# Moving low parts of weights and pooling operands from GpSimd to VectorE in a hybrid decoder layer

## The chip, the cores and the metric

The kernel runs on one core of one Trainium2 chip. The metric is the device time of one execution in microseconds. A core has five engines with instruction queues of their own, each worked off strictly in order: TensorE (PE, matrix products; PEld is its loading of weights), VectorE (DVE), ScalarE (ACT), GpSimd (POOL), and SyncE (SP), which here issues most transfers. An engine whose next instruction waits for another engine holds up everything behind that instruction.

## The reference

One decoder layer over 1024 tokens of width 1024, all in float32:

```python
z = h @ w_in                                   # split into pool group | q | k | v
y_pool = pool_mixer(u_pool, w_pool, pool_scale)
y_attn = sliding_window_attention(q, k, v, sinks)   # window 128, 8 query heads, 2 kv heads
mix = concat([y_pool, y_attn]) @ w_out
h = layer_norm(ALPHA * h + mix, ln1_g, ln1_b)
ff = square(relu(h @ w_ff1)) @ w_ff2
h = layer_norm(ALPHA * h + ff, ln2_g, ln2_b)
h = h + sigmoid(h @ w_ple_gate + b) * (p @ w_ple)

def pool_mixer(u, w_pool, pool_scale):         # four groups of 128 channels, windows 2, 4, 8, 16
    d = mean of the last `window` tokens - u   # fewer tokens at the sequence's start
    return (d @ w_pool[group]) * pool_scale
```

## The kernel before

Every float32 product is made of three fast ones. An operand is split into a high part, its value rounded to the matrix engine's own format, and a low part, the rest; `mm3` adds high x high, high x low and low x high. The high part is made by ScalarE (`high`, line 98, a copy with rounding) and the low part by `low` (line 103), a subtraction `source - high`, on an engine that the caller names. So a low part comes always after a cast by ScalarE.

Tokens lie in two halves of 512 (t = 0, 1). The first 300 us of the program hold these stages, interleaved:

- The input projection (`z_tile`): each block of 128 columns of `w_in` is loaded into a staging tile `st` (two buffers), split into `w` (two buffers), and multiplied with eight blocks of x.
- `attention(n)` for eight blocks of 128 queries, in two groups of heads each: scores (lines 289, 290, tile s), bias and row minimum on VectorE (line 293, tile e), exponential on ScalarE (line 300), reciprocal (304) and scaling (306) on VectorE, transposes (313, tile pt), split into pp, product with the values (318, 319, tile av), sum of its halves (321, 322, tile y), split into the `mixA` tiles (c). The low part of `mixA` is GpSimd's.
- `pooling`: for four groups in each half, the window sums (line 357, up to four additions of 512 to 527 columns) on GpSimd, the difference to the token (line 360, tile h) on VectorE, in the first half the correction of the first tokens (lines 365, 366) on GpSimd, then the split of the operand `dT` (tile `tmp`, one buffer) and its product with the group's matrix `wp`. The result is scaled into `mixP` (lines 100, 376).
- The output projection's left half of columns for the first four token blocks (`out_left(0, ...)`): its weights come in four pieces of 128x1024, staged in st and split into w (w_1757, w_1786, w_1815, w_1844 in the rows below); four accumulators (mm_1753 to mm_1755 and s_1756) take all eight k blocks, and `residual` (line 437) adds them to the residual rows n. Then the right half's weights `wo` (c_1984 and c_1993, two pieces each) for `out_right`, and `out_left(1, ...)`, whose weights (w_2118, w_2147 and two more) are split by VectorE already.

Then come the first layer norm (lines 399 to 415), the feed-forward layer as fewer block products (from about 300 us on), and the gate.

The order of the instructions on each engine is made by a scheduler that plays the program with its own estimates of durations when it is built; code order only breaks ties. A change of engine therefore moves other instructions too. Buffers are few: of the accumulators `mm` there are three, and a new one waits until an old one's reader is through.

Of the kernel before, what the change touches and what calls it, by code (L numbers as in the profile page):

```python
# [12 lines left out]
P = 128  # L13
D = 1024
S = 1024
HALF = 512
# [51 lines left out]
def layer(ctx, tc, xT, x, pT, w_in, w_pool, pscale, sinks, w_out, ln1, w1, w2, ln2, w_ple, w_gate, bgate, bias, rcount, out):  # L68
    nc = tc.nc
# [6 lines left out]
    def nm(s):  # L76
        uid[0] += 1
        return f"{s}_{uid[0]}"

    def big(shape, dt=F32R):  # L80
        return sb.tile(shape, dt, tag="c", bufs=6, name=nm("c"))

    def wt(shape, dt=F32R):
        return sb.tile(shape, dt, tag="w", bufs=2, name=nm("w"))
# [4 lines left out]
    def stage(shape):  # L89
        return sb.tile(shape, F32, tag="st", bufs=2, name=nm("st"))  # L90
# [5 lines left out]
    def high(dst, src, scale=None):  # L96
        if scale is None:
            nc.scalar.copy(out=dst, in_=src)  # L98
        else:
            nc.scalar.mul(out=dst, in_=src, mul=scale)  # L100

    def low(eng, dst, src, hi):
        return eng.tensor_tensor(out=dst, in0=src, in1=hi.bitcast(F32), op=ALU.subtract)  # L103

    def load_split(dst_h, dst_l, src, shape, eng, st=None):
        st = stage(shape) if st is None else st
        nc.sync.dma_start(out=st, in_=src)
        high(dst_h, st)
        low(eng, dst_l, st, dst_h)

    def mm3(o, ah, al, bh, bl, first, last, more=False):
        nc.tensor.matmul(o, ah, bh, start=first, stop=False, skip_group_check=more)  # L112
        nc.tensor.matmul(o, ah, bl, start=False, stop=False, skip_group_check=more)  # L113
        nc.tensor.matmul(o, al, bh, start=False, stop=last, skip_group_check=more)  # L114
# [30 lines left out]
    def tmp(shape, dt=F32):  # L145
        return pa.tile(shape, dt, tag="tmp", bufs=1, name=nm("tmp"))

    def row(shape, dt=F32):
        return pa.tile(shape, dt, tag="h", bufs=6, name=nm("h"))
# [14 lines left out]
    def acc_ps():  # L164
        return ps.tile([P, HALF], F32, tag="mm", bufs=3, name=nm("mm"))
# [172 lines left out]
    def pooling(n):  # L338
        for _ in range(n):
            while steps and len(ahead) < 2:  # L340
                gi, t = steps.pop(0)
                ahead.append((gi, t, z_tile(6 + gi, t)))
            pool_group(*ahead.pop(0))

    def pool_group(gi, t, o):
        win = WINDOWS[gi]
        u = row([P, PAD + HALF])
        nc.gpsimd.tensor_copy(out=u[:, 0:PAD], in_=halo[:, gi, :])
        nc.scalar.copy(out=u[:, PAD:], in_=o)
        if t == 0:  # L350
            nc.gpsimd.tensor_copy(out=halo[:, gi, :], in_=u[:, HALF : HALF + PAD])
        sums = [row([P, PAD + HALF]) for _ in range(2)]
        cur, a, side = 1, u, 0
        while cur < win:
            d0 = 2 * cur - 1
            b = sums[side]
            nc.gpsimd.tensor_tensor(out=b[:, d0:], in0=a[:, d0:], in1=a[:, d0 - cur : PAD + HALF - cur], op=ALU.add)  # L357
            a, side, cur = b, 1 - side, 2 * cur
        dd = sums[side][:, PAD:]
        nc.vector.scalar_tensor_tensor(  # L360
            out=dd, in0=a[:, PAD:], scalar=1.0 / win, in1=u[:, PAD:], op0=ALU.mult, op1=ALU.subtract
        )
        if t == 0:
            f = win - 1
            nc.gpsimd.tensor_tensor(out=dd[:, 0:f], in0=a[:, PAD : PAD + f], in1=rc[:, 0:f], op=ALU.mult)
            nc.gpsimd.tensor_tensor(out=dd[:, 0:f], in0=dd[:, 0:f], in1=u[:, PAD : PAD + f], op=ALU.subtract)
        dT = tmp([P, 2, HALF], F32R)
        high(dT[:, 0], dd)
        low(nc.gpsimd, dT[:, 1], dd, dT[:, 0])
        y = acc_ps()  # L370
        mm3(y, wp[:, 0, gi, :], wp[:, 1, gi, :], dT[:, 0], dT[:, 1], True, True)
        if mixP[t] is None:
            mixP[t] = big([P, 2, 4, HALF])
        m = mixP[t]
        high(m[:, 0, gi, :], y, psc[:, gi : gi + 1])
        nc.vector.scalar_tensor_tensor(
            out=m[:, 1, gi, :], in0=y, scalar=psc[:, gi : gi + 1], in1=m[:, 0, gi, :].bitcast(F32),
            op0=ALU.mult, op1=ALU.subtract,
        )
# [47 lines left out]
    def out_load(dst, dh, kk, st, eng):  # L427
        load_split(dst[:, 0], dst[:, 1], w_out[dh, kk], None, eng, st)

    def out_mm(o, n, k, w):  # L430
        m = (mixP if k < 4 else mixA)[n // 4]
        c = (n % 4) * P
        mm3(o, m[:, 0, k % 4, c : c + P], m[:, 1, k % 4, c : c + P], w[:, 0, k % 2, :], w[:, 1, k % 2, :], k == 0, k == NK - 1)
# [6 lines left out]
    def out_left(t, staging, eng, room=None):  # L440
        blocks = range(4 * t, 4 * t + 4)
        os = [acc_ps() for _ in range(3)]
        os.append(ps.tile([P, HALF], F32, tag="s", bufs=2, name=nm("s")))
        for k in range(NK):
            if k % 2 == 0:
                w = room[:, k // 2 - 2] if room is not None and k > 3 else wt([P, 2, 2, HALF])
                out_load(w, 0, k // 2, staging(), eng)
            for n in blocks:
                out_mm(os[n % 4], n, k, w)
        return os  # L450

    def residual_load(t):
        for n in range(4 * t, 4 * t + 4):
            hn[n] = nat([P, D])
            nc.sync.dma_start(out=hn[n], in_=x[n * P : (n + 1) * P, :])
# [35 lines left out]
    attention(6)  # L491
    pooling(2)
    residual_load(0)
    left = out_left(0, lambda: stage([P, 2, HALF]), nc.gpsimd)
    attention(7)
    residual_left(0, left)
    pa_ctx.close()
# [95 lines left out]
    for j in range(2):  # L593
        w = big([P, 2, 2, 2, HALF])
        for i in range(2):
            out_load(w[:, i], 1, 2 * j + i, stage([P, 2, HALF]), nc.gpsimd)
        wo.append(w)
    gb1 = [stage([P, D]) for _ in range(2)]
    for j in range(2):
# [368 lines left out]
```

## Time and profile before

| what | value |
|---|---|
| median of 3 runs | 1004.0 us (1003.68 to 1005.26) |
| profiled execution | 1003.74 us, span 1001.9 us, mean granted TensorE clock 0.996 |
| TensorE busy | 989.8 us (99%) |
| VectorE busy | 709.4 us (71%) |
| ScalarE busy | 459.0 us (46%) |
| GpSimd busy | 129.2 us (13%), 158 instructions |

In the profile, a line such as `L103 POOL TENSOR_TENSOR tmp<-h,tmp 128x512` is one group or one instruction: the source line (that of the helper `low`, so the tile's name tells which split it is), the engine, the operation, output and inputs, and partitions by elements. What stands in square brackets in a timeline is the idle time of that engine before the instruction and what ended it. In a row of waits, "PE av L319 <- DVE pp L103: 2.8, 2, 2.5" says that TensorE waited for VectorE 2.8 us in all, twice, 2.5 at the longest.

### The profile page before, as it was taken

How to read it: one execution, taken by the hardware profiler on the slowest of the kernel's cores; microseconds unless marked ns; L12 is line 12 of the kernel's file. 1: busy time of each engine (PE TensorE's matmuls, PEld its weight loads, DVE VectorE, ACT ScalarE, POOL GpSimd, SP SyncE). 2: the span in 40 equal slices, each digit the busy share in tenths (PEclk: the TensorE clock that was granted, in tenths of full speed). 3: DMA queues.
4: the chain of work that ended last, by engine and by line, in shares of the span. 5: the costliest groups of instructions: out<-in, count | busy, mean ns of one | idle time of the engine just before them, and what ended most of it. 6: DMA issues, size and time to landing. Idle time of an engine off the chain costs nothing.

```text
span 1001.9 us, 12220 instructions
## 1 busy us (share of the span) xinstructions
PE 989.8 (99%) x4562; PEld 822.2 (82%) x4562; DVE 709.4 (71%) x1121; ACT 459.0 (46%) x737; POOL 129.2 (13%) x158
## 2 busy tenths in 40 slices
PE   9999998999999999999999999999999999999998
PEld 7888886788888888888888888888888888888887
DVE  5889897666878876666446756887657699897333
ACT  5667766542576444344454433433433354651111
POOL 0031655430000000100000000100021110000000
PEclk9999998999999999999999999999999999999999
DMA  6524111452152433663264793775798773621011
GB/s 216 179 75 156 44 64 63 148 167 85 74 198 107 165 150 123 199 173 135 87 235 162 299 335 114 176 231 190 204 225 187 201 168 126 200 85 43 32 43 43
DMA packets 39004, 148.01 MB, mean 148 GB/s; under 512 B 4768, under 2 KB 5920, under 8 KB 36128
## 3 DMA queue, kind: packets, MB, share of 16 engines
q1 hardware_dynamic: 29952, 116.29, 33.6%
q0 software_dynamic: 7840, 26.74, 11.5%
q10 hardware_dynamic: 1152, 4.19, 1.0%
q8 instruction: 36, 0.59, 0.2%
q14 instruction: 24, 0.20, 0.1%
HBM read 124.66 MB, written 22.54 MB: 147 GB/s over the span
## 4 chain that ended last, share of the span: by engine, by line
PE 91%; DVE 5%; ACT 2%; POOL 1%; issue 1%; DMA 1%; SPq 0%; ACTq 0%; DVEq 0%; POOLq 0%
PE f L112 22%; PE f L114 22%; PE f L113 22%; PE mm L113 6%; PE mm L114 6%; PE mm L112 6%; DVE e L306 1%; PE pt L313 1%; PE f L424 1%; DVE e L293 1%; DVE pp L103 1%; POOL h L357 1%; PE av L319 1%; DMA n<-in_xT 1%; DVE h L360 1%
## 5 line engine op out<-in xcount | busy, mean ns | idle before, releaser
L112 PE MATMUL f<-c,ws 128*128 128x512 f32 (+1 forms) x456 | 175.8, 385 | 0.0
L113 PE MATMUL f<-c,ws 128*128 128x512 f32 (+1 forms) x456 | 175.7, 385 | 0.0
L114 PE MATMUL f<-c,ws 128*128 128x512 f32 (+1 forms) x456 | 175.2, 385 | 0.0
L113 PE MATMUL f<-x,w 128*128 128x512 f32 x448 | 174.3, 389 | 0.0
L114 PE MATMUL f<-x,w 128*128 128x512 f32 x448 | 174.3, 389 | 0.0
L112 PE MATMUL f<-x,w 128*128 128x512 f32 x448 | 147.1, 389 | 0.0
L98 ACT CAST w<-st 128x1024 fp32r<-128x1024 f32 (+2 forms) x66 | 65.7, 998 | 105.9 <-issue 69.8
L103 DVE TENSOR_TENSOR w<-st,w 128x1024 fp32r<-128x1024 f32 (+2 forms) x62 | 72.9, 1178 | 46.1 <-ACT w L98 46.0
L114 PEld LDWEIGHTS f<-c,ws 128*128 128x128 f32 x456 | 85.7, 188 | 17.2
L112 PEld LDWEIGHTS f<-c,ws 128*128 128x128 f32 x456 | 85.7, 188 | 17.1
L113 PEld LDWEIGHTS f<-c,ws 128*128 128x128 f32 x456 | 85.7, 188 | 17.0
L113 PEld LDWEIGHTS f<-x,w 128*128 128x128 f32 x448 | 84.1, 188 | 17.6
L114 PEld LDWEIGHTS f<-x,w 128*128 128x128 f32 x448 | 84.1, 188 | 17.4
L112 PEld LDWEIGHTS f<-x,w 128*128 128x128 f32 x448 | 84.1, 188 | 17.3
L98 ACT CAST ws<-w 128x512 fp32r<-128x512 f32 x60 | 37.1, 622 | 58.0 <-PE f L114 42.4
L103 DVE TENSOR_TENSOR x<-ws,x 128x1024 fp32r<-128x1024 f32 x52 | 63.4, 1219 | 0.0
L103 DVE TENSOR_TENSOR ws<-w,ws 128x512 fp32r<-128x512 f32 x60 | 41.2, 689 | 28.6 <-ACT ws L98 28.2
L117 DVE TENSOR_TENSOR n<-t,f 128x512 f32<-128x512 f32 x48 | 31.9, 685 | 39.3 <-PE f L114 39.2
L113 PE MATMUL mm<-c,w 128*128 128x512 f32 x144 | 56.9, 396 | 0.3 <-DVE c L103 0.3
L112 PE MATMUL mm<-c,w 128*128 128x512 f32 x144 | 56.7, 400 | 0.0
L114 PE MATMUL mm<-c,w 128*128 128x512 f32 x144 | 56.5, 395 | 0.0
L98 ACT CAST ws<-st 128x512 fp32r<-128x512 f32 x48 | 29.8, 621 | 58.1 <-PE f L114 35.2
(214 smaller groups left out, 1850.9 us busy)
## 6 DMA issues: line engine op xcount, KB each, us to landing
ws<-in_w SPq DMA_DIRECT2D x70, 512.0 KB, 3.6
w<-in_w SPq DMA_DIRECT2D x16, 1024.0 KB, 5.0
c<-fd SPq DMA_DIRECT2D x6, 2048.0 KB, 8.6
fd<-n POOLq DMA_DIRECT2D x20, 512.0 KB, 4.2
ws<-in_w POOLq DMA_DIRECT2D x20, 512.0 KB, 7.5
st<-in_w_in SPq DMA_DIRECT2D x17, 512.0 KB, 3.3
w<-in_w SPq DMA_DIRECT2D x10, 512.0 KB, 3.8
n<-in_x SPq DMA_DIRECT2D x8, 512.0 KB, 4.3
```

The lines of the kernel that those rows point to most:

```text
L98: nc.scalar.copy(out=dst, in_=src)
L103: return eng.tensor_tensor(out=dst, in0=src, in1=hi.bitcast(F32), op=ALU.subtract)
L112: nc.tensor.matmul(o, ah, bh, start=first, stop=False, skip_group_check=more)
L113: nc.tensor.matmul(o, ah, bl, start=False, stop=False, skip_group_check=more)
L114: nc.tensor.matmul(o, al, bh, start=False, stop=last, skip_group_check=more)
L117: nc.vector.tensor_tensor(out=o, in0=a, in1=b, op=op)
L293: nc.vector.tensor_tensor_reduce(out=e[:, 2 * j + i, k0 : 2 * P], in0=s[:, i, k0 : 2 * P], in1=nd[:, k0 : 2 * P], scale=-SLOPES[h], scalar ...
L306: nc.vector.tensor_scalar(out=e[:, i, k0 : 2 * P], in0=e[:, i, k0 : 2 * P], scalar1=st[:, 12 + i : 13 + i], scalar2=None, op0=ALU.mult)
L313: nc.tensor.transpose(pt[:, i, :], e[:, i, kb * P : (kb + 1) * P], ident)
L319: nc.tensor.matmul(av, VV[0][:, blk, g], pp[:, 1], start=False, stop=(kb == 1))
L357: nc.gpsimd.tensor_tensor(out=b[:, d0:], in0=a[:, d0:], in1=a[:, d0 - cur : PAD + HALF - cur], op=ALU.add)
L360: nc.vector.scalar_tensor_tensor(out=dd, in0=a[:, PAD:], scalar=1.0 / win, in1=u[:, PAD:], op0=ALU.mult, op1=ALU.subtract)
```

## The change

The engine of three groups of low parts is another: those of the pooling operands (eight of 128x512), of the weights of `out_left(0, ...)` (four of 128x1024) and of the right half's weights `wo` (four of 128x1024). GpSimd keeps the low parts of `wp` and of `mixA`, the window sums and the small copies.

```diff
@@ pool_group
         high(dT[:, 0], dd)
-        low(nc.gpsimd, dT[:, 1], dd, dT[:, 0])
+        low(nc.vector, dT[:, 1], dd, dT[:, 0])
@@ 
-    left = out_left(0, lambda: stage([P, 2, HALF]), nc.gpsimd)
+    left = out_left(0, lambda: stage([P, 2, HALF]), nc.vector)
@@ 
-            out_load(w[:, i], 1, 2 * j + i, stage([P, 2, HALF]), nc.gpsimd)
+            out_load(w[:, i], 1, 2 * j + i, stage([P, 2, HALF]), nc.vector)
```

The scheduler makes another order of it. Three places on VectorE show it. The first is a pooling group of the first half (h_1138 is the token tile, h_1142 its window sum, h_1143 the difference, tmp_1150 its split; e_1160 is an attention tile; w_1329 an input weight). Before:

```order
L322 TENSOR_TENSOR y_791<-av_868,yl_889 64x512
L103 TENSOR_TENSOR pp_997<-pt_992,pp_997 128x512
L360 SCALAR_TENSOR_TENSOR h_1143<-h_1142,h_1138 128x512
L103 TENSOR_TENSOR pp_1007<-pt_1002,pp_1007 128x512
L293 ISA e_1160,sm_1161<-s_1162,nd,sink_sb 128x256
```

and now:

```order
L322 TENSOR_TENSOR y_791<-av_868,yl_889 64x512
L103 TENSOR_TENSOR pp_1007<-pt_1002,pp_1007 128x512
L360 SCALAR_TENSOR_TENSOR h_1143<-h_1142,h_1138 128x512
L103 TENSOR_TENSOR tmp_1150<-h_1143,tmp_1150 128x512
L103 TENSOR_TENSOR w_1329<-st_1330,w_1329 128x1024
L293 ISA e_1160,sm_1161<-s_1173,nd,sink_sb 128x256
```

The low part of tmp_1150 stands directly behind the difference from which ScalarE must first make the high part; two groups of the second half (tmp_1521, tmp_1570) stand so too, and the other five have other work in between.

The second place is the end of the pooling, where the output projection begins (mm_1524, mm_1573 and mm_1723 are products of pooling groups, e_1580 and e_1630 attention tiles). Before:

```order
L376 SCALAR_TENSOR_TENSOR c_1528<-mm_1573,psc,c_1528 128x512
L360 SCALAR_TENSOR_TENSOR h_1715<-h_1716,h_1712 128x512
L304 RECIPROCAL sm_1631<-sm_1631 128x4
L306 TENSOR_SCALAR e_1630<-e_1630,sm_1631 128x256 x4
L322 TENSOR_TENSOR y_1378<-av_1455,yl_1476 64x512
L360 SCALAR_TENSOR_TENSOR h_1733<-h_1732,h_1729 128x512
L103 TENSOR_TENSOR pp_1612<-pt_1607,pp_1612 128x512
L103 TENSOR_TENSOR pp_1622<-pt_1617,pp_1622 128x512
```

and now:

```order
L103 TENSOR_TENSOR w_1757<-st_1758,w_1757 128x1024
L376 SCALAR_TENSOR_TENSOR c_1528<-mm_1524,psc,c_1528 128x512
L376 SCALAR_TENSOR_TENSOR c_1528<-mm_1573,psc,c_1528 128x512
L360 SCALAR_TENSOR_TENSOR h_1715<-h_1716,h_1712 128x512
L304 RECIPROCAL sm_1581<-sm_1581 128x4
L103 TENSOR_TENSOR pp_1461<-pt_1456,pp_1461 128x512
L306 TENSOR_SCALAR e_1580<-e_1580,sm_1581 128x256 x4
L103 TENSOR_TENSOR tmp_1720<-h_1715,tmp_1720 128x512
```

The last pooling groups now come one attention tile earlier, and the first output weight's low part is on VectorE ahead of them; w_1786's follows behind the two halves of e_1630's line 293, a y and a pp.

The third place is the change-over from the first output accumulators to the right half's weights. Before:

```order
L306 TENSOR_SCALAR e_1924<-e_1924,sm_1925 128x256 x4
L103 TENSOR_TENSOR w_2118<-n_2119,w_2118 128x1024
L322 TENSOR_TENSOR y_1873<-av_1900,yl_1921 64x512
L437 SCALAR_TENSOR_TENSOR n_1745<-n_1745,mm_1753 128x512
L437 SCALAR_TENSOR_TENSOR n_1747<-n_1747,mm_1754 128x512
```

and now:

```order
L103 TENSOR_TENSOR pp_1906<-pt_1901,pp_1906 128x512
L103 TENSOR_TENSOR pp_1916<-pt_1911,pp_1916 128x512
L103 TENSOR_TENSOR c_1984<-st_1985,c_1984 128x1024
L103 TENSOR_TENSOR c_1984<-st_1989,c_1984 128x1024
L103 TENSOR_TENSOR w_2118<-n_2119,w_2118 128x1024
L437 SCALAR_TENSOR_TENSOR n_1745<-n_1745,mm_1753 128x512
L103 TENSOR_TENSOR c_1993<-st_1994,c_1993 128x1024
L437 SCALAR_TENSOR_TENSOR n_1747<-n_1747,mm_1754 128x512
```

The residual that frees the first accumulator (mm_1753, whose buffer mm_2006 of the right half takes) now stands behind three low parts whose sources are still being loaded, and the second group of attention block 7 (e_1924's scaling) has moved behind this place, in front of the first layer norm. On TensorE the right half's first products (mm_2006) now come directly behind the first accumulators' last ones; before, a part of `out_left(1, ...)` with w_2118 stood in between.

## The prediction

> **What bounds the kernel now.** I read the page's engine row first, then the table by stage (columns: stretch, its length, busy time of TensorE, of its weight loads, of VectorE, ScalarE, GpSimd, then granted clock and transfers), then TensorE's own waits between 60 and 200 us, and last the timelines at those waits.
>
> ```profile
> PE 989.8 (99%) x4562; PEld 822.2 (82%) x4562; DVE 709.4 (71%) x1121; ACT 459.0 (46%) x737; POOL 129.2 (13%) x158
> 100.00:150.00 50.00, 49.56 (x273) 41.93 (x272) 42.99 (x93) 33.26 (x78) 29.33 (x39) 1.00 0.16 54
> 150.00:164.00 14.00, 12.10 (x57) 9.35 (x57) 11.77 (x29) 10.37 (x25) 8.84 (x9) 1.00 0.18 59
> 164.00:172.00 8.00, 5.34 (x18) 4.12 (x19) 6.76 (x12) 5.02 (x11) 5.38 (x5) 0.57 0.26 94
> 172.00:200.00 28.00, 26.77 (x131) 22.12 (x130) 16.83 (x35) 13.11 (x25) 11.80 (x5) 1.00 0.37 127
> 200.00:300.00 100.00, 100.00 (x470) 83.05 (x469) 71.86 (x139) 49.57 (x76) 14.90 (x15) 1.00 0.37 131
> ...
> PE av L319 <- DVE pp L103: 2.8, 2, 2.5
> PE mm L112 <- ACT tmp L98: 1.3, 2, 0.7
> PE pt L313 <- DVE e L306: 0.9, 1, 0.9
> PE mm L113 <- POOL tmp L103: 0.8, 1, 0.8
> PE av L318 <- DVE y L322: 0.5, 1, 0.5
> PE s L289 <- DVE sm L293: 0.4, 1, 0.4
> ```
>
> TensorE is the bound, so the change can give or take only TensorE's idle time and slow clock where the moved instructions lie. At stake in 150 to 172 us: 1.90 us idle, 2.66 us idle, and 5.34 us of work at a mean clock of 0.57, which costs 5.34 x 0.43 = 2.3 us; together 6.9 us. At 184 to 186 us, two waits (on e and sm) of 0.9 + 0.4: 1.2 us by the rows below. In 100 to 150 us only 0.44 us is idle, from 200 to 300 us none. At most 8.5 us can be gained, and a loss has no such limit.
>
> Of the waits only 0.8 us names GpSimd. Its larger part is indirect: VectorE stretched by what GpSimd does beside it. Timeline rows (start, length), VectorE first, then GpSimd at the same times, then TensorE:
>
> ```profile
> 107.23 0.68 DVE L360 SCALAR_TENSOR_TENSOR h<-h,h 128x512 f32<-128x512 f32 x1
> 125.11 1.21 DVE L103 TENSOR_TENSOR w<-st,w 128x1024 fp32r<-128x1024 f32 x1
> 153.62 3.11 DVE L306 TENSOR_SCALAR e<-e,sm 128x256 f32<-128x256 f32 x4
> 160.71 2.16 DVE L306 TENSOR_SCALAR e<-e,sm 128x256 f32<-128x256 f32 x4
> 164.08 2.58 DVE L360 SCALAR_TENSOR_TENSOR h<-h,h 128x512 f32<-128x512 f32 x1
> 181.94 3.30 DVE L306 TENSOR_SCALAR e<-e,sm 128x256 f32<-128x256 f32 x4
> 189.16 1.14 DVE L306 TENSOR_SCALAR e<-e,sm 128x256 f32<-128x256 f32 x4
> 193.69 2.58 DVE L103 TENSOR_TENSOR w<-n,w 128x1024 fp32r<-128x1024 f32 x1 [3.39 <-ACT w L98]
> ...
> 152.59 2.40 POOL L103 TENSOR_TENSOR w<-st,w 128x1024 fp32r<-128x1024 f32 x1
> 161.38 1.35 POOL L103 TENSOR_TENSOR tmp<-h,tmp 128x512 fp32r<-128x512 f32 x1 [4.86 <-ACT tmp L98]
> 163.76 2.35 POOL L103 TENSOR_TENSOR w<-st,w 128x1024 fp32r<-128x1024 f32 x1
> 182.72 4.76 POOL L103 TENSOR_TENSOR w<-st,w 128x1024 fp32r<-128x1024 f32 x2 [0.65 <-ACT w L98]
> 192.79 5.74 POOL L103 TENSOR_TENSOR c<-st,c 128x1024 fp32r<-128x1024 f32 x2 [5.31 <-ACT c L98]
> ...
> 167.31 0.79 PE L319 MATMUL av<-pp,k 128*128 128x512 f32 x1 [2.46 <-DVE pp L103]
> 172.63 0.39 PE L114 MATMUL mm<-w,c 128*128 128x512 f32 x1
> 174.67 0.39 PE L114 MATMUL mm<-w,c 128*128 128x512 f32 x1
> 185.30 0.44 PE L313 MATMUL pt<-ident,e 128*128 128x128 f32 x2 [0.86 <-DVE e L306]
> ```
>
> Four scalings (L306) take 1.14 us undisturbed at 189.16, but 3.11, 2.16 and 3.30 beside a low of tmp or w on GpSimd; the pooling difference (L360) takes 0.68 undisturbed and 2.58 beside the low of w at 163.76. TensorE's longest wait, 2.46 us at 167.31, is for an operand (pp) behind that stretched L360, and 0.86 us at 185.30 for the scalings behind the two lows at 182.72. All of these lows are moved.
>
> **The change part by part.** Prices: GpSimd's groups (60 to 215 us), then VectorE's (60 to 210 us).
>
> ```profile
> L103 POOL TENSOR_TENSOR tmp<-h,tmp 128x512 fp32r<-128x512 f32 x8 | 11.4, 1427 | 12.6 <-ACT tmp L98 12.6
> L103 POOL TENSOR_TENSOR c<-st,c 128x1024 fp32r<-128x1024 f32 x4 | 10.5, 2647 | 9.2 <-ACT c L98 9.2
> L103 POOL TENSOR_TENSOR w<-st,w 128x1024 fp32r<-128x1024 f32 x4 | 9.5, 2388 | 0.6 <-ACT w L98 0.6
> L357 POOL TENSOR_TENSOR h<-h 128x527 f32<-128x527 f32 x8 | 8.8, 1099 | 0.0
> ...
> L103 DVE TENSOR_TENSOR pp<-pt,pp 128x512 fp32r<-128x512 f32 x29 | 19.1, 682 | 3.7 <-ACT pp L98 3.6
> L103 DVE TENSOR_TENSOR w<-st,w 128x1024 fp32r<-128x1024 f32 x10 | 13.8, 1378 | 1.6 <-ACT w L98 1.5
> ```
>
> GpSimd loses 16 instructions and 31.4 us. VectorE gains 8 lows of tmp at 0.68 (nearest row: pp, same shape) and 8 of w and c at 1.21: 5.4 + 9.7 = 15.1 us. Relief from the rows above: 1.97 + 1.02 + 1.90 + 2.16 + 1.37 = 8.4 us. No transfer, cast or matmul is added.
>
> *100 to 172 us.* Seven lows of tmp and two of w fall here: 4.8 + 2.4 = 7.2 us, less the relief up to 164.08, 4.9 us: net +2.3. VectorE's idle time there is 72 - 61.5 (42.99 + 11.77 + 6.76) = 10.5 us. In two ways more of it goes.
>
> First, a low at the head of VectorE's queue waits for ScalarE's cast. In the new order tmp stands directly behind its L360 in three groups. For h_1143 these rows price it:
>
> ```profile
> 109.00 0.22 POOL L365 TENSOR_TENSOR h<-h,rc 128x7 f32<-128x7 f32 x1
> 109.83 0.62 ACT L98 CAST tmp<-h 128x512 fp32r<-128x512 f32 x1
> ```
>
> L360 ends at 107.91 and the cast at 110.45, since GpSimd's edge fix and ScalarE's queue lie between: a low of tmp directly behind L360 would wait 2.5 us there, with all that is queued behind it: the low of w_1329, two L293 and a pp. In the new order two L293 and a pp have moved ahead of that L360, so I take 2.0. The other two have no edge fix: the cast alone, 0.62, and some 0.13 of passing on: 0.75 each. Together 3.5 us.
>
> Second, the window sums (L357, 1.1 us each) stay on GpSimd and can hold up the moved lows, which read two tiles of SBUF as L360 does. Bounds: 0 (the row at 125.11) to a whole sum for each of nine, 9.9 us. The nearest rows are the ten lows of w, same instruction in the same stage: mean 1.38 against 1.21, 0.17 each. I take 0.2 x 9 = 1.8 us. VectorE is then left with 10.5 - 2.3 - 3.5 - 1.8 = 2.9 us of slack: it should keep up, narrowly.
>
> The Trainium skill, page "SBUF — State Buffer", section "Who interferes with whom", says that a VectorE instruction with two SBUF inputs contends with a GpSimd instruction that reads SBUF, and that whichever comes second waits for the whole of the first. L360 at 164.08 agrees; the 0.17 us of the ten w lows is far from a whole sum. If each low met one, the sum's 1.8 would be 9.9 us; that is the slower rival below.
>
> *What is left of the 6.9 us.* A matmul takes 2.04 / 9 = 0.227 us (rows 172.63 to 174.67). In the new order, between the transposes of e_1580 and the low of w_1786, TensorE has thirteen matmuls, four score matmuls of 0.12 and four transposes of 0.11: 3.9 us. VectorE has tmp_1720, four L293 with their reads (0.41 each), y, pp and the low: 3 x 0.6 + 1.6 + 1.2 = 4.6 us. So 0.7 us of waiting stays. The next cast of tmp follows L360 by 0.75, behind 1.1 us of matmuls: 0.3. One window sum across the path adds 1.1. Left: 2.1 us in short pieces, none as long as the 2.46 behind which the clock fell, so I let the 2.3 us of slow clock go too. Gain 6.9 - 2.1 = 4.8 us.
>
> *184 to 186 us.* No low is on GpSimd there; gain 1.2 us.
>
> *New losses.* In 100 to 150 us VectorE has 7.0 us idle and gets four tmp lows (2.7 us) and most of the 3.5 us of queue waiting; TensorE has projection matmuls to fill, but the slack is narrow and I charge 1.5 us. At the change-over to the right half, VectorE now makes the lows of c_1984 before w_2118 and before the residual that frees the accumulator for mm_2006:
>
> ```profile
> 187.30 1.22 SPq L107 DMA_DIRECT2D st<-in_w_out  x2
> 191.66 1.05 ACT L98 CAST c<-st 128x1024 fp32r<-128x1024 f32 x1 [2.75 <-DMA st<-in_w_out]
> ```
>
> From the end of w_1815's low: 2.5 us to that of w_1844, 4.4 to land (187.30 to 191.66), 1.05 for the cast, two lows, a residual of 0.7: 11.1 us. TensorE has 48 matmuls before it (10.9) and 1.4 us of attention: slack 1.2 us. I charge 0.5. Behind it the first layer norm now stands ahead of two pp lows on VectorE and waits on GpSimd's power and ScalarE; TensorE has 23 matmuls (5.2 us) there: charge 0.8. Everything later stays covered by TensorE's 100% from 200 us on.
>
> *Sum:* -4.8 - 1.2 + 1.5 + 0.5 + 0.8 = -3.2 us. The profiled execution took 1003.74 (span 1001.9, 1.84 around it): 1000.5. The median, 1004.0, lies 0.26 above that execution: **1000.8 us**.
>
> **The rivals.**
> 1. *Slower: window sums hold up the moved lows.* Before this charge VectorE has 4.7 us of slack in 100 to 172 us, so it decides from 4.7 / 9 = 0.52 us a low. At the whole 1.1 us TensorE loses 9.9 - 4.7 = 5.2 us and the stalls of 150 to 172 us stay: 1004.0 - 1.2 + 5.2 = 1008.0; at 0.8 each, 1005.3. For it: 164.08 shows such a stretch. Against: the w lows show 0.17.
> 2. *No change to be seen.* The attention chain (exponentials, scalings, pp) was late anyway and stalls TensorE again with another name; only the 0.8 us that names GpSimd goes, and 184 to 186 us is paid back at the change-over: 1004.0 - 0.8 = 1003.2. For it: 4.2 of the 5.0 us of waits there name VectorE or ScalarE, and tmp's cast is not moved. Against: the stretched rows that made them late.
> 3. *Nearly all is gained.* No new stall: 1004.0 - 8.1 = 995.9. For it: GpSimd's sums too finish sooner. Against: the 0.7 us worked out above.
>
> That the lows would not move is excluded by the program's order.
>
> **How the numbers follow.** My forecast 0.42 (its own range 998.5 to 1002), nearly all gained 0.10, no change 0.25, slower 0.23. Within 0.2%, 1002.0 to 1006.0, a measurement can hardly tell a change. So faster 0.52, same 0.25, slower 0.23. The range 997 to 1006 leaves out about half of the third rival (0.05) and somewhat over half of the slower case (0.13).
>
> **What would show it.** Right: GpSimd under 100 us busy; the L306 blocks near 1.1 us; clock 1.00 throughout 150 to 190; TensorE idle under 3 us from 100 to 200; 16 more lows on VectorE at 0.7 and 1.2. Wrong: lows of tmp over 1.2 us beside L357 (rival 1); waits on pp or e of 4 us or more in total between 150 and 175, and a clock dip (rival 2); a wait for c_1984 or its accumulator near 195 to 200 us; new idle time between 205 and 225.

## The result and the profile after

The changed kernel takes 998.85 us in the median of six runs (997.1 to 999.47) against 1004.4 us of the kernel before on the same chips (six runs, 1003.68 to 1005.49): ratio 0.9941 [0.9928, 0.9954], 5.5 us or 0.6% faster. The prediction was 1000.8 us, faster.

The profiled execution of after took 999.47 us, the longest of the six, with a span of 997.7 us: 4.2 us less than before's 1001.9. First its engine row on the page, then the table by stage, with the columns of the prediction's table (stretch, length, TensorE, weight loads, VectorE, ScalarE, GpSimd, granted clock, transfers). The first two rows and the fourth and fifth matter most.

```profile
PE 988.8 (99%) x4562; PEld 821.3 (82%) x4562; DVE 712.1 (71%) x1137; ACT 458.8 (46%) x737; POOL 103.5 (10%) x142
```

```profile
0.00:60.00 60.00, 57.53 (x264) 47.27 (x265) 41.56 (x81) 38.15 (x73) 5.01 (x13) 1.00 0.52 175
60.00:100.00 40.00, 37.89 (x188) 31.25 (x187) 31.39 (x82) 24.24 (x58) 10.12 (x12) 0.96 0.33 117
100.00:150.00 50.00, 50.00 (x267) 42.26 (x266) 42.85 (x102) 33.81 (x79) 26.44 (x35) 1.00 0.18 64
150.00:164.00 14.00, 14.00 (x79) 11.90 (x78) 13.23 (x34) 12.60 (x30) 6.20 (x7) 1.00 0.11 38
164.00:172.00 8.00, 8.00 (x41) 6.41 (x39) 6.27 (x16) 4.90 (x13) 1.60 (x2) 1.00 0.37 133
172.00:200.00 28.00, 27.50 (x135) 22.84 (x134) 21.83 (x41) 16.53 (x29) 1.48 (x2) 1.00 0.57 197
200.00:300.00 100.00, 100.00 (x475) 83.09 (x474) 77.26 (x146) 50.50 (x80) 10.90 (x14) 1.00 0.32 117
```

From 150 to 172 us TensorE now never idles and the granted clock is 1.00: all 6.9 us that stood at stake there are gone (1.90 + 2.66 idle, 2.3 of slow clock). From 100 to 150 us 0.44 us of idle time went, from 172 to 200 us 0.73. Against that stands the second row. Before, the first two rows were:

```profile
0.00:60.00 60.00, 58.29 (x270) 48.44 (x270) 42.25 (x83) 38.15 (x73) 5.02 (x13) 1.00 0.53 177
60.00:100.00 40.00, 39.61 (x208) 33.40 (x207) 35.47 (x92) 28.66 (x69) 11.72 (x15) 1.00 0.35 126
```

So between 60 and 100 us 1.72 us of TensorE are lost as idle time, and the clock fell as well. The rows of TensorE's timeline with those idle pieces, and the clock in stretches of 2 us right after them:

```profile
89.04 0.39 PE L289 MATMUL s<-k,n 128*128 128x256 f32 x1 [0.84 <-DVE sm L293]
90.64 0.50 PE L318 MATMUL av<-pp,k 128*128 128x512 f32 x1 [0.86 <-ACT pp L98]
```

```profile
90.00:92.00 2.00, 1.36 (x6) 1.01 (x7) 1.97 (x8) 2.00 (x7) 0.00 (x0) 0.94 0.46 127
92.00:94.00 2.00, 2.00 (x5) 1.53 (x5) 1.97 (x6) 1.04 (x5) 0.00 (x0) 0.50 1.01 367
94.00:96.00 2.00, 2.00 (x8) 1.62 (x7) 1.97 (x7) 0.00 (x0) 0.00 (x0) 0.71 0.99 385
```

The slow clock costs 1.36 x 0.06 + 2.00 x 0.50 + 2.00 x 0.29 = 1.7 us. The sum over the stages, by idle time and clock: +0.76 (0 to 60 us, a late first operand, which differs from run to run) + 1.72 + 1.7 - 0.44 - 1.90 - 2.66 - 2.3 - 0.73 = -3.9 us, of a measured -4.2.

How VectorE was relieved is seen in its groups from 60 to 210 us (count, busy us and mean ns of one, idle time before):

```profile
L306 DVE TENSOR_SCALAR e<-e,sm 128x256 f32<-128x256 f32 x56 | 18.6, 393 | 0.3
L103 DVE TENSOR_TENSOR tmp<-h,tmp 128x512 fp32r<-128x512 f32 x8 | 5.5, 685 | 3.8 <-ACT tmp L98 3.8
L360 DVE SCALAR_TENSOR_TENSOR h<-h,h 128x512 f32<-128x512 f32 x8 | 5.4, 680 | 0.1
L103 DVE TENSOR_TENSOR w<-st,w 128x1024 fp32r<-128x1024 f32 x14 | 18.6, 1327 | 2.8 <-ACT w L98 2.8
```

In the kernel before, the first and third read:

```profile
L306 DVE TENSOR_SCALAR e<-e,sm 128x256 f32<-128x256 f32 x56 | 27.3, 548 | 0.5
L360 DVE SCALAR_TENSOR_TENSOR h<-h,h 128x512 f32<-128x512 f32 x8 | 8.0, 998 | 0.1
```

The scalings lost 8.7 us of busy time and the pooling differences 2.6. The eight new lows of tmp cost 5.5 us. VectorE's busy time over the whole run grew by only 2.7 us (709.4 to 712.1) although it makes 16 more instructions.

### The profile page after: what moved, and what is told of

The parts are those of the page before. It is cut to its first block, busy times and chain, and to the rows that moved or that the text cites. A ratio compares the mean times of both kernels' runs of the same rounds, so it can differ in the third digit from the quotient of the medians.

```text
span 997.7 us, 12217 instructions
## 1 busy us (share of the span) xinstructions
PE 988.8 (99%) x4562; PEld 821.3 (82%) x4562; DVE 712.1 (71%) x1137; ACT 458.8 (46%) x737; POOL 103.5 (10%) x142
## 3 DMA queue, kind: packets, MB, share of 16 engines
q0 software_dynamic: 7840, 26.74, 11.3%
## 4 chain that ended last, share of the span: by engine, by line
PE 96%; ACT 1%; POOL 1%; DMA 1%; DVE 0%; SPq 0%; issue 0%; DVEq 0%; ACTq 0%; POOLq 0%
PE f L112 23%; PE f L114 23%; PE f L113 23%; PE mm L112 8%; PE mm L113 7%; PE mm L114 7%; PE pt L313 1%; PE f L424 1%; PE s L290 1%; PE s L289 1%; PE av L319 1%; PE av L318 1%; DMA n<-in_xT 1%; POOL h L357 1%; PE s L114 0%; PE s L113 0%
## 5 line engine op out<-in xcount | busy, mean ns | idle before, releaser
L103 DVE TENSOR_TENSOR w<-st,w 128x1024 fp32r<-128x1024 f32 (+2 forms) x66 | 77.7, 1180 | 46.6 <-ACT w L98 46.6
L112 PE MATMUL mm<-c,w 128*128 128x512 f32 x144 | 58.3, 409 | 0.8 <-ACT c L98 0.7
L113 PE MATMUL mm<-c,w 128*128 128x512 f32 x144 | 57.2, 398 | 0.3 <-DVE c L103 0.3
L114 PE MATMUL mm<-c,w 128*128 128x512 f32 x144 | 57.0, 398 | 0.0
```

## The experiments

Three explanations were open. **A, relief:** GpSimd's subtractions hold VectorE up while both read, so taking them off GpSimd shortens VectorE's other work. **B, latency:** a low on VectorE takes about half as long (0.68 against 1.43 us, 1.21 against 2.39), so TensorE has its operand sooner. **C, list:** the scheduler writes another order of instructions, and gain or loss comes from that order. A table of all timed kernels first; each was compared with the kernel before on the same chip (medians 1004.27 in the first four rows, 1004.54 in the next three, 1004.52 in the last four).

| run | made by VectorE | median us (lowest to highest) | ratio to before |
|---|---|---|---|
| e1_pool | pooling operands only | 1001.44 (1000.3 to 1002.16) | 0.9972 [0.9961, 0.9982] |
| e2_left | the four left weights only | 996.82 (996.53 to 997.89) | 0.9931 [0.9918, 0.9943] |
| e6_leftright | left and right weights | 996.32 (996.2 to 997.12) | 0.9925 [0.9913, 0.9938] |
| e4_first | all of the change but one pooling operand | 1001.7 (999.75 to 1003.76) | 0.9975 [0.9964, 0.9987] |
| e7_beside | as e6, four reading subtractions added per left weight on GpSimd | 1000.79 (1000.23 to 1002.76) | 0.9967 [0.9955, 0.998] |
| e8_mix | as e6, and mixA's lows | 995.42 (995.14 to 996.13) | 0.9912 [0.9898, 0.9925] |
| e9_second | as e6, and pooling operands of the second half | 996.93 (996.6 to 997.36) | 0.9927 [0.9913, 0.994] |
| e11_set | as e6, eight fills added per left weight on GpSimd | 996.82 (996.34 to 997.06) | 0.9923 [0.9911, 0.9936] |
| e10_firsthalf | as e6, and pooling operands of the first half | 997.63 (995.9 to 997.84) | 0.9929 [0.9917, 0.9942] |
| e3_right | the four right weights only | 1004.5 (1003.65 to 1005.59) | 0.9999 [0.9991, 1.0008] |
| e5_mix | the whole change, and mixA's lows | 998.14 (998.04 to 998.5) | 0.9938 [0.9924, 0.9952] |

### One part at a time

**e1_pool**: of the change only

```diff
-        low(nc.gpsimd, dT[:, 1], dd, dT[:, 0])
+        low(nc.vector, dT[:, 1], dd, dT[:, 0])
```

> Only the eight low parts of the pooling operands are moved to VectorE; those of the output weights stay on GpSimd. Theory A (relief: GpSimd's subtractions hold VectorE up while they run): the weights' lows on GpSimd go on stretching the scalings and differences of VectorE near 153, 164 and 182 us, so only part is gained: 1000.5 to 1002.5 us, the wait at 184 to 186 us of about 1 us stays, L306 has a mean of over 450 ns between 60 and 210 us. Theory B (latency: a low of 0.68 us instead of 1.3 reaches TensorE sooner): all of the pooling part is gained, 998 to 1000 us. Theory C (the new list of instructions alone is better, whatever the engines do): no relation to either; near 999 if the list is like that of the whole change.

Measured: 2.8 us faster, inside the range given for A. The stalls that remain name GpSimd. TensorE's longest waits, 60 to 200 us:

```profile
PE mm L113 <- POOL w L103: 1.1, 1, 1.1
PE s L113 <- POOL w L103: 1.1, 1, 1.1
PE av L318 <- ACT pp L98: 0.9, 1, 0.9
PE s L289 <- DVE sm L293: 0.8, 1, 0.8
```

The last two are the early pair at 89 and 91 us; it comes with the pooling lows alone. The scalings fell only to 443 ns, the pooling differences to 952, and the eight lows of tmp take 808 ns here, against 685 in after.

**e2_left**: only

```diff
-    left = out_left(0, lambda: stage([P, 2, HALF]), nc.gpsimd)
+    left = out_left(0, lambda: stage([P, 2, HALF]), nc.vector)
```

> Only the four low parts of the output projection's left weights (first accumulators) are moved to VectorE. Theory A (relief): three of the four long stretches go (153.6, 164.1 and 181.9 us), so most of the 6.9 us at 150 to 172 us and the 1.2 us at 184 to 186 us is gained: 999 to 1001 us. Theory B (latency): the low parts of the pooling operands, for which TensorE waited, come as late as before: 1002.5 to 1004.5 us. Theory C (list): no relation.

Measured: 7.4 us faster, more than the whole change and 2.2 us below the range given for A. Moving four instructions is enough for it. The table by stage:

```profile
60.00:100.00 40.00, 39.63 (x208) 33.40 (x207) 35.45 (x92) 28.63 (x69) 11.71 (x15) 1.00 0.34 124
150.00:164.00 14.00, 12.57 (x62) 10.31 (x62) 13.16 (x32) 11.82 (x27) 7.44 (x8) 1.00 0.12 40
164.00:172.00 8.00, 8.00 (x41) 6.59 (x40) 5.52 (x12) 4.22 (x10) 2.77 (x3) 1.00 0.36 129
```

No early pair, a clock of 1.00 in these stretches, and from 150 to 164 us 1.43 us of idle time left. B has little to give here: in the kernel before TensorE's one wait for GpSimd was for a low of tmp (0.8 us), none for a low of w.

**e3_right**: only

```diff
-            out_load(w[:, i], 1, 2 * j + i, stage([P, 2, HALF]), nc.gpsimd)
+            out_load(w[:, i], 1, 2 * j + i, stage([P, 2, HALF]), nc.vector)
```

> Only the four lows of the right half's weights on VectorE; left half and pooling stay on GpSimd as before. The relief theory gives the 1.2 us of waits at 184 to 186 us and nothing else: 1002.8 to 1003.8, with the stalls of 150 to 172 us as in the kernel before. A list theory allows anything between 1000 and 1006. Latency (a low of 1.2 us in place of 2.4) gives at most the same 1.2 us.

Measured: nothing, and that was a miss. The two lows at 182.7 us, behind which the scalings wait, are of the left weights; the right half's come from 192 us on, where TensorE has work in hand. The rows of VectorE and TensorE there are still those of before:

```profile
181.96 3.30 DVE L306 TENSOR_SCALAR e<-e,sm 128x256 f32<-128x256 f32 x4
185.32 0.44 PE L313 MATMUL pt<-ident,e 128*128 128x128 f32 x2 [0.83 <-DVE e L306]
```

**e6_leftright**: both weight edits, the pooling line as before.

> The low parts of both halves of the output weights are moved, those of the pooling operands stay on GpSimd. Theory A (relief): within 0.7 us of the kernel with the left half alone, since TensorE has no idle time from 190 to 300 us where the right half's lows lie. Theory B (latency): 1002.5 to 1004.5 us. If the right half has a part of its own, it is over 1 us from the left half alone.

Measured: 996.32, 0.5 us below e2_left with overlapping ranges. So the weights are worth about 8 us and the pooling part, added to them, takes back 2.5 (998.85 against 996.32, each beside a before within 0.13 us of the other).

### Relief or latency

**e7_beside**: e6, and behind each left weight's cast GpSimd subtracts the high part from itself in four pieces into a scratch tile that nobody reads. VectorE's part of the work is the same.

```diff
+        if beside is not None:
+            for i in range(4):
+                h = dst[:, 0, i // 2, i % 2 * 256 : i % 2 * 256 + 256].bitcast(F32)
+                nc.gpsimd.tensor_tensor(out=beside, in0=h, in1=h, op=ALU.subtract)
```

> Both halves of the output weights on VectorE (996.3 us), with four extra GpSimd subtractions of 128x256 beside each of the four low parts of the left half: they read the weights' high part and write to a scratch tile that nobody reads, so GpSimd is as busy there as it was in the kernel before, and VectorE's list of instructions stays nearly the same. Theory A (GpSimd's subtractions hold VectorE up while they run, and delay the pooling operands behind them on GpSimd): the stretched scalings and differences come back and with them the stalls at 150 to 172 us: 1000 to 1004 us. Theory B (the gain was that the weights' low parts reach TensorE sooner) and theory C (the list): VectorE still makes those, in the same list, so 996 to 997.5 us.

Measured: 1000.79, 4.5 us above e6. The lows are still short and on VectorE, yet 4.5 of the 7.9 us gained are lost again. (In the profiled executions 1.2 us of the difference lies before 60 us, where the kernels are alike; e11, next, has the same late start, 57.13 us busy against 56.90, and is the cleaner partner.)

**e11_set**: e7, but GpSimd fills the scratch tile instead, eight times 128x256, behind one subtraction of two columns that keeps it in the same place.

```diff
-            for i in range(4):
-                h = dst[:, 0, i // 2, i % 2 * 256 : i % 2 * 256 + 256].bitcast(F32)
-                nc.gpsimd.tensor_tensor(out=beside, in0=h, in1=h, op=ALU.subtract)
+            h = dst[:, 0, 0, 0:2].bitcast(F32)
+            nc.gpsimd.tensor_tensor(out=beside[:, 0:2], in0=h, in1=h, op=ALU.subtract)
+            for i in range(8):
+                nc.gpsimd.memset(beside, 0.0)
```

> Both weight halves' low parts on VectorE, the pooling operands' lows on GpSimd, and beside each of the four left weights GpSimd now does one tiny subtraction (two columns) and eight fills of 128x256 that read nothing, in place of the four subtractions of the earlier control. If what cost 4.5 us there was that GpSimd's instructions read SBUF while VectorE reads two tiles (relief theory), most of it goes: 996.3 to 998, with the scalings L306 within 10% of 469 ns or a little over. If it was that GpSimd's own queue came late to its next pooling low, or the changed order of instructions (list theory), about the same remains: 1000 to 1002.

Measured: 996.82, within 0.5 us of e6. GpSimd is about as busy as in e7 (11.81 and 4.15 us in the two stretches, against 11.11 and 5.10), and costs hardly anything when it reads nothing. The 4.0 us between the two medians are the price of the reading. Order can hardly be it: by the programs' order TensorE, VectorE and ScalarE have in e11 exactly the lists of e6. In e7 seven of TensorE's matmuls and two neighbouring pairs of VectorE's instructions and one of ScalarE's stand elsewhere, but ahead of the stall on the second left weight's low (164.65 us in e7, 163.64 in e11) both do the same work. The table by stage, 150 to 172 us, of e7_beside and then of e11_set:

```profile
150.00:164.00 14.00, 12.00 (x57) 9.57 (x57) 13.00 (x30) 10.86 (x26) 11.11 (x14) 1.00 0.11 37
164.00:172.00 8.00, 7.36 (x28) 5.77 (x29) 5.74 (x11) 3.41 (x9) 5.10 (x5) 0.79 0.35 133
```

```profile
150.00:164.00 14.00, 11.88 (x60) 9.76 (x60) 13.16 (x31) 11.77 (x26) 11.81 (x22) 1.00 0.11 37
164.00:172.00 8.00, 8.00 (x41) 6.56 (x40) 5.97 (x13) 4.69 (x10) 4.15 (x8) 1.00 0.38 133
```

VectorE's timeline shows where the difference arises. First e7_beside, then e11_set, the same pieces of work:

```profile
156.35 1.06 DVE L306 TENSOR_SCALAR e<-e,sm 128x256 f32<-128x256 f32 x2
161.15 2.31 DVE L306 TENSOR_SCALAR e<-e,sm 128x256 f32<-128x256 f32 x4
164.51 1.09 DVE L360 SCALAR_TENSOR_TENSOR h<-h,h 128x512 f32<-128x512 f32 x1
```

```profile
156.20 0.73 DVE L306 TENSOR_SCALAR e<-e,sm 128x256 f32<-128x256 f32 x2
160.50 1.95 DVE L306 TENSOR_SCALAR e<-e,sm 128x256 f32<-128x256 f32 x4
163.51 0.68 DVE L360 SCALAR_TENSOR_TENSOR h<-h,h 128x512 f32<-128x512 f32 x1
```

Each piece is 0.3 to 0.4 us shorter in e11, and so is a pair of scalings just before them (0.69 us against 1.11). The second left weight's low comes at 163.38 us in e7 and at 162.37 in e11, though e11 was 0.27 behind at the first (152.17 against 151.90): of these 1.28 us, the three groups of scalings make 0.42 + 0.33 + 0.36 = 1.1. With 1.77 us of waiting for that low in the one and 1.4 in the other, the clock falls to 0.79 in the one and not in the other. So the price contains some 1.5 us of slow clock behind the longer wait (7.36 x 0.21).

**m1_beside** measures the pairs alone. It leaves the whole layer out: sixteen VectorE instructions of each kind, by themselves, then with as many GpSimd additions (128x512) beside them, then with fills.

```python
    for pool in (None, pool_sum, pool_set):
        for what in (scaling, difference, low_weight, low_psum):
            sync()
            for i in range(N):
                what(i)
                if pool is not None:
                    pool(i)
```

> Not the layer: sixteen of each of four VectorE instructions (scaling in place 128x256, difference of two SBUF tiles 128x512, low part of a weight 128x1024, low part with one input in PSUM 128x512) are timed alone, then beside GpSimd additions of 128x512 like the window sums, then beside GpSimd memsets of 128x512. By the traces so far: alone 0.27, 0.6, 1.14 and 0.6 us from start to start. Beside the additions the first three should be held up by a good part of the addition's 1.1 us, the one with an input in PSUM not at all. If only a reading GpSimd instruction holds up the two-input forms, the memsets leave them alone; the scaling may differ.

VectorE's timeline, alone (first four rows) and beside additions (next four), the scaling beside fills (ninth), then GpSimd's additions beside the weight low and beside the PSUM form:

```profile
10.33 4.28 DVE L39 TENSOR_SCALAR e<-e,sc 128x256 f32<-128x256 f32 x16
15.56 11.59 DVE L42 SCALAR_TENSOR_TENSOR lo<-h,u 128x512 f32<-128x512 f32 x16
28.15 20.13 DVE L45 TENSOR_TENSOR lo<-st,hi 128x1024 fp32r<-128x1024 f32 x16
49.35 11.57 DVE L48 TENSOR_TENSOR lo<-pt,u 128x512 fp32r<-128x512 f32 x16
61.87 19.31 DVE L39 TENSOR_SCALAR e<-e,sc 128x256 f32<-128x256 f32 x16
84.59 24.77 DVE L42 SCALAR_TENSOR_TENSOR lo<-h,u 128x512 f32<-128x512 f32 x16
112.77 34.23 DVE L45 TENSOR_TENSOR lo<-st,hi 128x1024 fp32r<-128x1024 f32 x16
149.13 11.57 DVE L48 TENSOR_TENSOR lo<-pt,u 128x512 fp32r<-128x512 f32 x16
171.60 7.08 DVE L39 TENSOR_SCALAR e<-e,sc 128x256 f32<-128x256 f32 x16
...
113.00 35.12 POOL L51 TENSOR_TENSOR gc<-ga,gb 128x512 f32<-128x512 f32 x16
149.29 21.42 POOL L51 TENSOR_TENSOR gc<-ga,gb 128x512 f32<-128x512 f32 x16
```

One instruction by itself and beside an addition: scaling 0.27 and 1.21 us, difference 0.72 and 1.55, weight low 1.26 and 2.14, and the form whose first input lies in PSUM 0.72 and 0.72. Beside fills the two-input forms keep their time (11.59 and 20.12 us for sixteen), and the scaling goes from 0.27 to 0.44. GpSimd can pay too: its addition takes 21.42 / 16 = 1.34 us beside the PSUM form and the same beside the scaling (21.38 for sixteen), but 35.12 / 16 = 2.20 beside the weight low.

The three runs agree: A is shown, as a cost of GpSimd's reading beside VectorE's, for 4.0 us, about half of what the weights gain. B is not the cause of these, since e7 has the same short lows as e11. For the other half A is likely but not shown. The short pieces of e7 hold VectorE up less than the long lows of the kernel before did: the work at these places (two times four scalings and a pooling difference) takes 3.11 + 2.16 + 2.58 = 7.85 us in before, 1.11 + 1.06 + 2.31 + 1.09 = 5.57 in e7 and 0.69 + 0.73 + 1.95 + 0.68 = 4.05 in e11. But e7's lists also differ from before's, and no run parts the two for this half.

### The order of the list, and where the pooling part loses

**e4_first**: the whole change, but the low of the pooling group that comes first in the program (group 3 of the first half) stays on GpSimd, to remove the early pair.

```diff
-        low(nc.vector, dT[:, 1], dd, dT[:, 0])
+        low(nc.gpsimd if (gi, t) == (3, 0) else nc.vector, dT[:, 1], dd, dT[:, 0])
```

> The whole change, but the first pooling group's low part (first half, window 16) stays on GpSimd. In the changed kernel TensorE lost 1.7 us of idle time at 88 to 92 us and then ran at half clock to 95 us, behind scalings and scores that this low part and its cast had pushed back on VectorE by 1.3 us. If that is the cause, this stall and the slow clock go and the rest stays: 995.5 to 997.5 us with a clock of 0.999 to 1.000. If the stall comes from the list as a whole, it appears again or elsewhere: 998.5 to 1000 us.

Measured: 1001.7, a miss by over 4 us, and above the range given for the list as well. The trace is of the slowest of its seven executions (1003.76; the fastest took 999.75), and about 2.6 of the 4.3 us by which it exceeds after's lie before 60 us, where the lists are the same. The pair is gone (39.62 us busy from 60 to 100), but over 600 places of TensorE's list differ from after's, and new waits stand at 153 to 170 us:

```profile
PE mm L112 <- ACT tmp L98: 1.9, 1, 1.9
PE s L113 <- DVE w L103: 1.4, 1, 1.4
PE s L289 <- DVE sm L293: 0.8, 1, 0.8
```

The clock was 0.86 from 164 to 172 us. An edit of one instruction of 1.3 us moved the time by 2.9 us. Explanation C fits that best; part of it is contention again (the seven lows of tmp on VectorE take 804 ns here against 685 in after, 0.8 us in all), and this run does not part the two further.

**e9_second** and **e10_firsthalf**: e6, and the pooling operands of one half of the tokens.

```diff
-        low(nc.gpsimd, dT[:, 1], dd, dT[:, 0])
+        low(nc.gpsimd if t == 0 else nc.vector, dT[:, 1], dd, dT[:, 0])    # e9; e10: the reverse
```

> Both halves of the output weights on VectorE, and of the pooling operands those of the second half of the tokens alone (four); the first half's, near which the changed kernel lost 3.2 us at 88 to 95 us, stay on GpSimd. If that early stall was all that the pooling part cost, this has the best of both: no stall at 88 to 95 us, and the waits of 0.7 us (cast of a pooling operand, 150 us) and 1.2 us (low of a weight, 163 us) that the kernel with the weights alone kept are less: 994.5 to 996.5 us. If moving pooling operands costs VectorE more than it saves anywhere: 997 to 999 us.

> Both weight halves' lows on VectorE and of the pooling operands' lows only the four of the first row half; the second half's four stay on GpSimd. If the 2.5 us that the whole change loses against the weights alone belong to the first half's lows (the idle pieces at 88 to 91 us behind the first moved low of tmp and the clock dip after them), they come back: 998 to 999.5, with waits on sm and pp of about 0.8 each between 88 and 91 us. If they came only from the whole change's particular order of instructions: 996 to 997, and no idle time there.

Measured: 996.93 and 997.63, both hardly to be told from e6's 996.32; e9 lies just above the best range given for it (994.5 to 996.5). Their tables from 60 to 100 us, e9_second first:

```profile
60.00:100.00 40.00, 39.62 (x210) 33.44 (x209) 35.45 (x91) 28.23 (x67) 11.72 (x15) 1.00 0.35 125
```

```profile
60.00:100.00 40.00, 37.91 (x191) 31.45 (x191) 31.55 (x81) 25.15 (x59) 10.11 (x12) 0.96 0.32 115
150.00:164.00 14.00, 14.00 (x79) 11.92 (x78) 13.89 (x35) 13.20 (x33) 8.42 (x9) 1.00 0.12 37
```

The early loss comes with the first half's lows and only with them, so e10's place was expected rightly; its sum was not. Its time was expected at 998 or more, but 150 to 164 us is full in e10 (14.00) and was 12.39 in e6, so 1.6 of the 3.4 us come back later.

Why the pair arises can be read in TensorE's order. Before:

```
L114 MATMUL mm_784<-tmp_781,wp 128x512
...
L289 MATMUL s_974<-k_256,n_317 128x256
L290 MATMUL s_974<-k_256,n_317 128x256
L112 MATMUL mm_934<-c_109,w_929 128x512
...
L318 MATMUL av_818<-pp_824,k_270 128x512
L289 MATMUL s_1017<-k_256,n_368 128x256
```

and in after, as in e10_firsthalf:

```
L114 MATMUL mm_784<-tmp_781,wp 128x512
...
L289 MATMUL s_974<-k_256,n_317 128x256
L290 MATMUL s_974<-k_256,n_317 128x256
L289 MATMUL s_1017<-k_256,n_368 128x256
...
L318 MATMUL av_818<-pp_824,k_270 128x512
...
L112 MATMUL mm_934<-c_109,w_929 128x512
```

The scores of the next tile and the first product with the values now stand ahead of the projection by w_929, which used to fill the time until VectorE and ScalarE had their operands. w_929's low is made at 80.72 us, 8 us before the pair, so the filler was ready; it only stands behind. The four kernels with this order (after, e1, e5, e10) have the pair, and the nine others, all with the old order here, have not; among these is e4, with seven of the eight lows of tmp on VectorE. But the new order comes exactly with the first pooling group's low on VectorE. That the order and not this low's load makes the pair is read from the lists; no run has the one without the other.

**e8_mix** and **e5_mix**: mixA's lows on VectorE too, on top of e6 and on top of the whole change.

```diff
-        low(nc.gpsimd, m[:, 1, :, c : c + P], yt, m[:, 0, :, c : c + P])
+        low(nc.vector, m[:, 1, :, c : c + P], yt, m[:, 0, :, c : c + P])
```

> Both halves of the output weights and the low parts of the attention output on VectorE; GpSimd keeps the pooling operands and the window sums. Theory A: eight subtractions of 1.3 us less on GpSimd relieve VectorE by up to 1 us each where a scaling lies beside them, at a price of 0.7 us each on VectorE, most of it where TensorE has no idle time: 994.5 to 997.5 us. If VectorE has no slack left, slower: 998 us or more.

> The whole change, and the four lows of the attention half of the mixed input (line 329) on VectorE too, which brought 0.9 us on top of the weights alone. If the idle time and clock dip at 88 to 95 us come from the first moved low of tmp, they stay whatever is done at line 329: 998 to 999. If that loss is one of the particular order of instructions: anything from 995.4 up.

e8_mix is the fastest kernel, 995.42 us, 9.1 below the kernel before. Against e6 the intervals of the ratios overlap, so a gain over it of 0.9 us is not settled. In e5_mix the early pair stays, at 0.52 and 0.73 us, without a dip of the clock.

## Why the prediction was right

The forecast held in sign and range: 998.85 against 1000.8. Point by point:

- **The bound and the places.** Right: the gain lies at 150 to 172 us and comes from VectorE's relief. The prediction took 1.97 + 1.02 + 2.16 = 5.15 us for L306 and 1.90 for L360, from four rows; over 60 to 210 us they fell by 8.7 and 2.6, together 11.3 against 7.05, so the relief was taken too small. (One reading in it was loose: of the 1.97 us at 153.62, 0.86 belong to the last scaling, 1.15 us long, which stood beside a window sum at 154.95, and no window sum was moved.) e7, e11 and m1 show the mechanism, for about half of the weights' gain.
- **"Gain 4.8 of 6.9": mis-sized.** All 6.9 us went. The 2.1 us of waits charged for the new order (0.7 + 0.3 + 1.1) did not appear. For the 0.7 both lengths were right: 3.9 us on TensorE (161.53 to 165.46) and 4.6 on VectorE (tmp_1720 at 159.85 to the end of w_1786's low at 164.4). The common start was wrong: TensorE came to the transposes only at 161.17, with matmuls to do until then, so the low was ready 1 us ahead of its use.
- **Window sums against the moved lows, 1.8 us: mis-sized, by nearly its whole amount.** Of the nine moved lows of 100 to 172 us only two overlap a window sum at all: the tmp at 133.48, where the sum paid (1.37 us, 1.07 undisturbed), and the w at 154.97 (1.32 against 1.21). So it cost VectorE 0.1 us, and the slower rival, which decided from 0.52 us a low, was far off. This is in part luck of the list: the lows of tmp have a mean of 685 ns here, but 808 in e1 and 804 in e4, and the first left weight's low takes 2.02 us in e6 and e11.
- **A low at its queue's head, 3.5 us.** Right: VectorE idles 3.8 us ahead of tmp, in three places, 2.3 at the longest. None of it reached TensorE in 100 to 150 us, so the charge of 1.5 was not needed.
- **184 to 186 us, 1.2.** Gone as said, though 0.50 us of waiting for c came at 176 us. The prediction's term did not say which lows did it; e3, which moves only the right half's and keeps the wait, shows that they are the left weights'.
- **Change-over and layer norm, 0.5 + 0.8.** Neither appeared: 27.50 of 28 us busy, then 100.
- **Not foreseen: 60 to 100 us.** The prediction looked at the order where stalls were and left 60 to 100 us alone. There the changed list costs 1.72 + 1.7 = 3.4 us.
- **One of its signs failed.** GpSimd was to be under 100 us busy and is at 103.5. It lost the lows, but its other work grew, from 60 to 215 us the window sums by 2.0 us and the small copies (L298, L348) by 2.3.

So the errors partly cancel, and that the forecast came within 2 us is in part luck. Against the predicted -3.2 us, charges of 2.1 + 1.5 + 0.5 + 0.8 = 4.9 were not needed and 0.44 more came from 100 to 150 us; 3.4 were lost early, 0.5 at 176 us and 0.76 at the start: -3.2 - 4.9 - 0.44 + 3.4 + 0.5 + 0.76 = -3.9, as the stages gave. The medians lie further apart (5.5) than the profiled executions (4.3), since that of after is 0.6 us above its median and that of before 0.7 below the one of its six runs.

The prediction weighed the Trainium skill's page "SBUF — State Buffer", section "Who interferes with whom". Its rule on which forms contend is borne out by m1: two inputs in SBUF beside a reading instruction contend (0.72 to 1.55), a PSUM input doesn't, a fill doesn't; a scaling contends even with a fill (0.27 to 0.44). The page lists the scaling's form (`tensor_scalar`) among those that can take the pair of ports that VectorE shares with GpSimd. What is paid is not the whole of the other instruction each time: a weight low and an addition side by side need 2.2 us, where one after the other they would need 1.26 + 1.34 = 2.60. Had the rule been charged at a full sum for each moved low, it would have given 9.9 us; in the kernel it was 0.1, since the list seldom set the two side by side.

## What to carry to other kernels

When GpSimd shares elementwise work with a nearly full VectorE, count what its reading instructions add to VectorE's own, from stretched rows against undisturbed ones of the same line: here moving four subtractions of 2.4 us off GpSimd gained 7.4 us, and GpSimd reads put back in their place cost 4.0 by stretching VectorE's other work. Move the parts one at a time, since the part that looked alike (the pooling operands) took back 2.5 us. After any such edit compare the bound engine's list over its whole length, not only at the old stalls.

## What the runs showed of the hardware

- A GpSimd fill beside VectorE costs a two-input form nothing (11.59 us for sixteen differences with and without), where an addition beside each more than doubles it (24.77). Inside the layer, swapping reading for filling was worth 4.0 us (1000.79 to 996.82).
- The granted clock can fall after two short idle pieces, 0.84 and 0.86 us ending 1.6 us apart: 0.50 at 92 to 94 us in after and 0.56 at 90 to 92 us in e10. It need not: nearly the same pieces at the same place in e1_pool, 0.80 and 0.85 us (0.93 us busy from 88 to 90, 1.42 from 90 to 92), left it at 1.00, and so did 0.52 and 0.73 us in e5_mix. So the length of the pieces doesn't settle it, and no run shows what does. In the six executions of after the mean clock was 0.998 in four and 0.999 and 1.000 in two, and these two took 997.1 and 997.66 us against 998.8 to 999.5; of the five of e10 the one at 1.000 took 995.9 and the others, at 0.998, 997.4 to 997.8.
- One wait of 1.19 us at 163 us (e6) and one of 1.41 us (e11) left the clock at 1.00; after one of 1.77 us (e7) at nearly the same place it was 0.79 from 164 to 172 us. The Trainium skill, page "TensorE: Matmul & The Clock Gate", section "Part 1: The HAM clock gate (the "warmup" mystery)", names in its table of the two states an idle window of about 3.4 us as what lowers the clock; further on it tells of another kernel in which short idle times between groups of matmuls did so. In after TensorE was busy for 0.93 us from 88 to 90 and for 1.36 us from 90 to 92, so here the clock fell without a window that is idle throughout.
